# Output projection from the second half of W_out, with its first tiles and gates reordered and the last tile's norm moved among the MLP's sets

## The chip, the core and the metric

The kernel runs on one core of a Trainium2 chip. A core has five engines, each with its own in-order instruction queue: TensorE (PE in the profile; its weight loads are PEld), VectorE (DVE), ScalarE (ACT), GpSimd (POOL) and SyncE (SP). They meet only through semaphores. PE writes to PSUM, from which DVE and ACT read; everything else lies in SBUF. DMA transfers are issued from an engine's queue (here nearly all from SP's) and are carried by 16 shared DMA engines. An instruction that waits holds up everything behind it on its own queue and nothing else. In this kernel the order on every queue is the order in which the Python code issues the instructions.

The metric is device time in microseconds. Before the change it was 3015.29 us, the median of three runs (3013.46 to 3018.35).

## What is computed

One layer of a diffusion backbone, for 256 context tokens and 2048 latent tokens (2304 tokens, 18 tiles of 128). Attention and a Fourier mixing give 512 columns each; this case is about what comes after them:

```python
def merge(attn, four, subln_g, lam_init, w_out):
    a = rms_norm(attn, subln_g) * (1.0 - lam_init)
    return jnp.concatenate([a.reshape(b, n, ATTN_WIDTH), four], axis=-1) @ w_out

mix = merge(attn, fourier_mix(f, w_four[l]), subln_g[l], lam_init, w_out[l])
xs = xs + g1 * mix
h = rms_norm(xs, norm2_g[l]) * (1 + sc2) + sh2
xs = xs + g2 * sq_relu_mlp(h, w1[l], w2[l])        # square(relu(h @ w1)) @ w2
```

The model width is 1024, the MLP's inner width 4096. The context tokens have their own modulation vectors (index `s` = 1, the latent tokens `s` = 0).

## The kernel before, in words

All products are float32 at high accuracy: each operand is split into a rounded part ("h" or "hi", by a cast on ACT or DVE) and the remainder ("l" or "lo", by a subtraction on DVE), and three matmuls replace one (`mm3`, lines 85 to 88).

**Attention** ends first. The last group of rows of the last head transposes its probabilities on PE (`tr`, line 972), splits them (`ah` on ACT, `al` on DVE) and multiplies them with V (`mul`). Then `o1` copies the result out of PSUM, `o2` transposes it back, `o3` copies it to SBUF, `o4` to `o6` normalize it (two squares on ACT, a step on DVE, a power and two scalings on POOL) and store it to `att`. These steps are put in an event list with due times and are sorted by them. W_out (8 blocks `WOUT[k]` of 128 x 1024) has been loaded long before into buffers of a head that is done.

**Output projection** (lines 1304 to 1449). The 18 token tiles go in the order `seq` = 0, 9, 1, 10, ..., 8, 17, so that tile t and tile t + 9 follow each other; the prediction calls the first three s0, s1 and s2. The parts of a tile:

- `mix_load(i)` issues three loads on SP: x (`xo`), the attention part (`am`) and the Fourier part (`mT`).
- `mix(i)` transposes `am` (4 transposes into `pmx`, line 1343), ACT scales that into `mT`, DVE makes `mh` and `ml` (lines 1347 and 1348).
- `w_split(hf)` makes the two parts of one half (512 columns) of W_out: 8 casts on ACT (`woh`), 8 subtractions on DVE (`wol`).
- `out_mm(i, hf)`: 24 matmuls of 128x512, eight k-blocks of three, into one of three PSUM tiles `po`.
- `mk_gate` builds the gate g1 as a row on all partitions: per half 4 matmuls into the single PSUM tile `pg` and a copy on ACT.
- `out_post(i, hf)`: two DVE operations, gate times product and the sum with x. `x_store` writes the new x, `x_norm` makes its RMS norm (ACT square, DVE, POOL power, DVE scaling to `xn`).
- `finish(i)`: 8 transposes of `xn` (`ptb`, line 199), 8 ACT operations to `hTb`; after tile t + 9 POOL makes four sums `ht` of the pair's quarters, and SP stores seven operands `hd` for the MLP.

Before, the first tiles are issued in the order: loads of s0 and s1, `w_split(0)`, `mix(s0)`, `out_mm(s0, 0)`, both halves of the context gate, `mix(s1)`, `w_split(1)`, loads of s2, `out_mm(s1, 0)`, both halves of the other gate, `out_mm(s0, 1)`, and then the loop. Four tiles before the last, the MLP's first loads are put on SP together: two sets of w1 blocks (`w_load`, four loads of 256 KB each, tile `a`) and three operands (`h_load`, 768 KB each, tile `hr`).

**MLP, first product** (lines 1452 to 1665). It uses a scheme with seven products in place of eight per pair of blocks. `ITEMS` lists them: for each set q of hidden columns the products p = 1, 6, (3 of the set before), 2, 7, 5, 4. One product is 12 matmuls of 128x384 (`mms`, lines 1492 to 1494). Products 1 and 2 share PSUM bank A, 6 and 7 bank B, 5 and 3 bank C. The later of two accumulates onto the earlier, so it must wait until the earlier one's result has been read (`post`: `us` on ACT for p = 1, `u` on DVE for p = 6). The weights need sums of blocks (`w_add`, `ws`, DVE), a cast (`w_cast`, ACT) and a remainder (`w_low`, DVE); the operands a cast (`mhh`) and a remainder (`mhl`) once per third of the tokens (`h_prep`). `mlp_ahead` does the first of these among the last tile's output projection.

The last tile's norm and its four sums are not done in the output projection but in `fin_norm` to `fin_store`, at the items 1, 3, 4, 6 and 7 of the MLP; their result is needed only in the last third of the tokens.

**Places.** Tile pools are laid out as two stacks, and a pool that lies where an earlier one lay makes each new tile wait for the readers of the old tiles underneath. Before, the first half of W_out's parts lies in the pool that is opened last on the left side, the second half just behind the working tiles.

## Time and profile before

| | us |
|---|---|
| median of three runs | 3015.29 |
| lowest, highest | 3013.46, 3018.35 |
| profiled execution, its own time | 3011.0 |
| span of that execution in the trace | 3009.2 |

| engine | busy us | share of the span |
|---|---|---|
| PE | 2922.0 | 97% |
| DVE | 2010.9 | 67% |
| ACT | 1568.6 | 52% |
| POOL | 1029.1 | 34% |

In the trace, attention's last matmul starts at 1324.95 us, the output projection's first transpose at 1326.07, the MLP's first matmul at 1582.65, and the last matmul into bank A at 2291.9.

How to read the views: the *timeline* gives start, duration, engine, line, and output <- inputs, with the idle time of that engine ahead of it and what ended it in brackets. The *waits* sum such idle times by who was waited for: total us, times, longest. The *windows* give the engines' busy us in a stretch, then the granted PE clock as a part of full speed (PEclk), the DMA engines' busy share and GB/s. Names are those of the program without numbers. One row of the timeline can hold several like instructions (x8); its duration is then that of the run of them. A matmul's duration includes its way through the array, so that successive ones overlap; the step from one start to the next is what it costs.

### The profile page before, as it was taken

The numbers are of one execution on the slowest core, as the hardware profiler recorded it, in microseconds if no ns is written. First come the engines' busy times: TensorE is split into PE (matmuls) and PEld (weight loads), VectorE is DVE, ScalarE is ACT, GpSimd is POOL, SyncE is SP. The second block draws the span as 40 slices with busy tenths as digits, with TensorE's granted clock in tenths as the row PEclk, the third lists the DMA queues.
The fourth block names the chain that finished last, engine by engine and source line by source line (L and its number), as shares of the span: only waits on it lengthen the run. The fifth ranks groups of instructions, "written<-read, shape, count | busy, mean of one in ns | idle before, by whom it ended". The sixth has DMA issues, their size and how long they took to land.

```text
span 3009.2 us, 43765 instructions
## 1 busy us (share of the span) xinstructions
PE 2922.0 (97%) x15417; PEld 2528.2 (84%) x15417; DVE 2010.9 (67%) x3375; ACT 1568.6 (52%) x3540; POOL 1029.1 (34%) x843
## 2 busy tenths in 40 slices
PE   8999999899999999989998999999999999999999
PEld 5888887678888888877878999999998888888887
DVE  6667775688888888864448777777775335344554
ACT  4333322688888888853336556556555322232221
POOL 1111112189888898831222333333332000000000
PEclk9999999999999999999999999999999999999999
DMA  7777878421121212114676676676666454444563
GB/s 271 208 190 207 221 192 256 176 101 33 46 107 34 107 38 87 32 50 161 199 224 211 229 241 214 213 230 222 222 199 212 150 166 163 131 155 164 200 218 105
DMA packets 394414, 495.58 MB, mean 165 GB/s; under 512 B 26403, under 2 KB 307056, under 8 KB 391122
## 3 DMA queue, kind: packets, MB, share of 16 engines
q1 hardware_dynamic: 386560, 477.63, 49.7%
q0 software_dynamic: 2992, 7.28, 0.8%
q10 hardware_dynamic: 4642, 7.88, 0.8%
q8 instruction: 122, 2.00, 0.3%
q14 instruction: 98, 0.80, 0.1%
HBM read 315.20 MB, written 179.57 MB: 164 GB/s over the span
## 4 chain that ended last, share of the span: by engine, by line
PE 82%; ACT 8%; DVE 4%; DMA 2%; issue 1%; SPq 1%; POOL 0%; ACTq 0%; DVEq 0%; POOLq 0%
PE Ss L916 8%; PE ps L87 8%; PE ps L86 8%; PE ps L88 8%; PE pj L87 4%; PE pj L88 4%; PE pj L86 4%; PE pts L972 3%; ACT P1s L940 3%; PE pB L1492 2%; PE pB L1494 2%; PE pB L1493 2%; PE pA L1492 2%; PE pA L1493 2%; PE pA L1494 2%; PE pC L1494 2%
## 5 line engine op out<-in xcount | busy, mean ns | idle before, releaser
L921 DVE TENSOR_REDUCE mxs<-Ss 128x1 f32<-128x512 f32 x640 | 419.1, 687 | 87.7 <-PE Ss L916 77.2
L1222 DVE TENSOR_TENSOR sl<-sr,sh 128x768 fp32r<-128x768 f32 x168 | 161.0, 959 | 349.4 <-ACT sh L1221 341.2
L963 POOL TENSOR_TENSOR P0s<-P0s,P1s 128x1024 f32<-128x1024 f32 x124 | 365.3, 2946 | 10.3
L1221 ACT CAST sh<-sr 128x768 fp32r<-128x768 f32 x168 | 140.1, 835 | 432.0 <-PE ps L87 432.0
L940 ACT ACTIVATE P1s<-Ss,mxs 128x512 f32<-128x512 f32 x320 | 217.2, 693 | 70.7 <-DVE mxs L924 70.7
L86 PE MATMUL pj<-wh,hh 128*128 128x512 f32 x576 | 229.3, 398 | 0.7 <-ACT fo L374 0.7
L87 PE MATMUL ps<-tlT,sh 128*128 128x512 f32 x585 | 229.3, 392 | 0.0
L86 PE MATMUL ps<-thT,sh 128*128 128x512 f32 x585 | 229.2, 392 | 0.0
L87 PE MATMUL pj<-wl,hh 128*128 128x512 f32 x576 | 227.8, 395 | 0.5 <-DVE wl L496 0.5
L88 PE MATMUL ps<-thT,sl 128*128 128x512 f32 x585 | 227.7, 389 | 0.0
L88 PE MATMUL pj<-wh,hl 128*128 128x512 f32 x576 | 226.5, 394 | 0.0
L1534 POOL TENSOR_TENSOR gs<-g,g 128x384 f32<-128x384 f32 x48 | 70.8, 1475 | 449.9 <-ACT g L1504 389.6
L940 ACT ACTIVATE P0s<-Ss,mxs 128x512 f32<-128x512 f32 x320 | 215.8, 696 | 7.5 <-DVE mxs L924 7.3
L916 PE MATMUL Ss<-KS1s,Qs 128*128 128x512 f32 x640 | 200.8, 427 | 11.4 <-ACT P0s L940 9.6
L916 PE MATMUL Ss<-KS0s,Qs 128*128 128x512 f32 x640 | 197.9, 421 | 10.7 <-ACT P1s L940 9.6
L972 PEld LDWEIGHTS pts<-ident,P0s 128*128 128x128 f32 x1280 | 157.1, 140 | 53.3 <-PE Ss L916 5.6
L972 PE MATMUL pts<-ident,P0s 128*128 128x128 f32 x1280 | 191.8, 273 | 7.4 <-DVE alp L1069 4.0
L1503 ACT ACTIVATE g<-uz 128x384 f32<-128x384 f32 x144 | 75.8, 527 | 207.4 <-DVE uz L1526 183.1
L87 PE MATMUL ps<-oplT,sh 128*128 128x512 f32 x423 | 166.9, 395 | 4.9 <-DVE oplT L1209 4.9
L962 POOL TENSOR_SCALAR P1s<-P1s,tots 128x1024 f32<-128x1024 f32 x124 | 166.7, 1344 | 5.6
L983 DVE TENSOR_TENSOR als<-pts,ahs 128x512 fp32r<-128x512 f32 x256 | 163.8, 681 | 5.4 <-ACT ahs L978 5.3
L86 PE MATMUL ps<-ophT,sh 128*128 128x512 f32 x423 | 166.9, 394 | 0.4 <-DVE uz L1526 0.4
(611 smaller groups left out, 8234.2 us busy)
## 6 DMA issues: line engine op xcount, KB each, us to landing
sr<-sd SPq DMA_DIRECT2D x84, 768.0 KB, 4.5
a<-in_w SPq DMA_DIRECT2D x184, 256.0 KB, 3.8
sd<-gs SPq DMA_DIRECT2D x192, 192.0 KB, 1.9
sd<-g SPq DMA_DIRECT2D x144, 192.0 KB, 4.3
wm<-in_w_mod SPq DMA_DIRECT2D x32, 512.0 KB, 5.0
Qs<-qd SPq DMA_DIRECT2D x32, 512.0 KB, 3.8
b<-in_w SPq DMA_DIRECT2D x64, 256.0 KB, 4.9
b<-tsum SPq DMA_DIRECT2D x64, 256.0 KB, 4.8
```

The source lines that it names most:

```text
L86: nc.tensor.matmul(ps, lh, rh, start=first, stop=False)
L87: nc.tensor.matmul(ps, lh, rl, start=False, stop=False)
L88: nc.tensor.matmul(ps, ll, rh, start=False, stop=last)
L916: nc.tensor.matmul(S[:, :w], self.Q[:, x, m, j * P:j * P + P], self.hd.KS[m][:, b * 512:b * 512 + w], start=(x == 0), stop=(x == 1))
L921: nc.vector.tensor_reduce(self.mx[j][:, m, b:b + 1], self.S[j, m, b], axis=AX.X, op=ALU.max)
L940: nc.scalar.activation(dst, S, AF.Exp, bias=self.mx[j][:, m, 6:7], accum_out=self.sm[j][:, m, b:b + 1])
L962: nc.gpsimd.tensor_scalar(p, p, tot[:, 3:4], 0.0, op0=ALU.mult, op1=ALU.add)
L963: nc.gpsimd.tensor_add(d, d, p)
L972: nc.tensor.transpose(pt[:, c:c + P], self.p0[j][:, (kb + t) * P:(kb + t + 1) * P], ident)
L983: nc.vector.tensor_sub(t, self.pt[kb], f32(self.A[kb][0]))
L1222: nc.vector.tensor_sub(lo, src, f32(hi))
L1494: nc.tensor.matmul(ps, wl[:, c], hh[:, k, :], start=False, stop=k == 3, skip_group_check=True)
```

## The change

- Attention's last group: its `o`, `osq`, `oss` and `s0e` tiles come from another pool, and its steps `o4` to `o6` leave the event list (`LASTO`). They are issued after the first 12 matmuls of the output projection.
- The output projection begins with the second half of W_out. Its parts lie in two pools of their own (`o_wh`, `o_wl`), the mixes in `o_m`, gates and norms in `o_g`. The loads of x are split off (`x_load`) and issued after those of `am` and `mT`. The weights are made in the order in which the matmuls use them: the first block's cast, `mix(s0)` with that block's remainder between `mh` and `ml`, then the other seven blocks. The first half of W_out is made later.
- The gates are built one half at a time, each ahead of its use. Both halves of s0 and s1 are done before the loop.
- The MLP's first loads are spread over the tiles 11 to 15 of the sequence instead of all at tile 14; at tile 15 `w_load(1)` comes after the last tile's loads.
- In the last tile `out_post(i, 0)` comes ahead of `mlp_ahead(0)`, and `mlp_ahead` has three parts; the first set's fourth sum is made there in place.
- The MLP's operands have a pool for each p, in the order 3, 4, 5, 2, 7.
- In the MLP's first items the casts follow a list (`CASTS`), `post(0, 6)` comes ahead of the sums of weights, the sums for the next set move from p = 6 and 2 to p = 7 and 5, and the load of set 2 from p = 7 to p = 5.
- The last tile's norm, transposes, load, sums and stores move from the items 1 to 7 to the items 10 to 22, in smaller pieces; the sums go from POOL to DVE.

```diff
-                    for t, fn in ((0, gr.o1), (0.4, gr.o2), (0.75, gr.o3), (2.32, gr.o4), (3.557, gr.o5), (4.0, gr.o6)):
-                        add(w + t * u, fn)
+                        if gr.last and t > 2:
+                            LASTO.append(fn)
+                        else:
+                            add(w + t * u, fn)
...
-            pool = hpa if p in (1, 6) else hp
+            pool = hpa if p in (1, 6) else hp[p]
...
-                w_cast(2)
-                w_low()
-            else:
+            elif part == 1:
                 for n in range(2):
                     h_load(0, ORDER[n + 3])
+                w_cast(2)
                 w_cast(3)
+            else:
                 w_low()
+                R = RAW[0]
+                nc.vector.tensor_sub(R["a12"], R["a12"], R["s2"])
+                R["s4"] = R["a12"]
...
+            tm = c4.enter_context(tc.tile_pool(name="o_m", bufs=2, reuse_waits="tile"))
+            wl1 = c4.enter_context(tc.tile_pool(name="o_wl", bufs=1, reuse_waits="tile"))
             t4 = c4.enter_context(tc.tile_pool(name="o_t", bufs=2, reuse_waits="tile"))
-            wp = c4.enter_context(tc.tile_pool(name="o_w", bufs=1, reuse_waits="tile"))
+            wh1 = c4.enter_context(tc.tile_pool(name="o_wh", bufs=1, reuse_waits="tile"))
+            tg = c4.enter_context(tc.tile_pool(name="o_g", bufs=2, reuse_waits="tile"))
...
-                mix_load(seq[0])
-                mix_load(seq[1])
+                mix_load(s0)
+                mix_load(s1)
+                x_load(s0)
+                x_load(s1)
+                nc.scalar.copy(WO[1][0][0], WOUT[0][:, 512:1024])
+                mix(s0, lambda: nc.vector.tensor_sub(WO[1][1][0], WOUT[0][:, 512:1024], f32(WO[1][0][0])))
+                w_split(1, 1)
+                out_mm(s0, 1, 0, 4)
+                for fn in LASTO:
+                    fn()
+                mix(s1)
+                out_mm(s0, 1, 4)
+                mk_gate(pp, g1[1], 16, 1, (1,))
                 w_split(0)
-                mix(seq[0])
-                out_mm(seq[0], 0)
-                mk_gate(pp, g1[1], 16, 1)
-                mix(seq[1])
-                w_split(1)
                 kv_even.close()
...
+                mix_load(s2)
+                x_load(s2)
+                out_mm(s1, 1)
+                mk_gate(pp, g1[0], 16, 0, (1,))
+                out_post(s0, 1)
+                out_mm(s0, 0)
+                mk_gate(pp, g1[1], 16, 1, (0,))
+                out_post(s1, 1)
+                mix(s2)
+                out_post(s0, 0)
+                x_store(s0)
+                x_norm(s0)
+                mix_load(seq[3])
+                x_load(seq[3])
+                out_mm(s1, 0)
+                mk_gate(pp, g1[0], 16, 0, (0,))
+                out_post(s1, 0)
+                x_store(s1)
+                x_norm(s1)
+                finish(s0)
+                for n, i in enumerate(seq[2:], 2):
...
-                    if n == N4 - 4:
+                    if n == N4 - 7:
                         w_load(0)
-                        for p in ORDER[:3]:
-                            h_load(0, p)
-                        w_load(1)
+                    if n in (N4 - 6, N4 - 5, N4 - 4):
+                        h_load(0, ORDER[n - N4 + 6])
                     if n == N4 - 3:
                         w_ahead()
+                        w_load(1)
...
-            hp = c5.enter_context(tc.tile_pool(name="m_h", bufs=1, reuse_waits="tile"))
+            hp.update((p, c5.enter_context(tc.tile_pool(name=f"m_h{p}", bufs=1, reuse_waits="tile"))) for p in (3, 4, 5, 2, 7))
...
-                nc.gpsimd.tensor_sub(T[:, 0], b12, b11)
-                nc.gpsimd.tensor_sub(T[:, 1], b22, T[:, 0])
...
+                    nc.vector.tensor_sub(T[:, 0], b12, b11)
+                    nc.vector.tensor_sub(T[:, 1], b22, T[:, 0])
...
-            FINISH = {1: (fin_norm,), 3: (fin_T,), 4: (fin_load,), 6: (fin_sums,), 7: (fin_store,)}
+            FINISH = {10: (fin_norm, ()), 12: (fin_scale, ()), 13: (fin_T, (0,)), 14: (fin_T, (1,)), 15: (fin_T, (2,)),
+                      16: (fin_load, ()), 19: (fin_sums, (0,)), 21: (fin_sums, (1,)), 22: (fin_store, ())}
+            CASTS = ((), (4,), (5,), (8, 6), (7,), (9,), (10, 11))
...
+                    early = q == 0 and p == 6
+                    if early:
+                        post(q, p, ps)
                     nw = q + 1
-                    if p == 1 and wset(q) == q:
+                    if q and p == 1 and wset(q) == q:
                         w_add(q, 3)
                     if nw < NQ and wset(nw) == nw:
-                        for x in {6: (0, 1), 2: (2,)}.get(p, ()):
+                        for x in ({7: (0, 1), 5: (2,)} if q == 0 else {6: (0, 1), 2: (2,)}).get(p, ()):
                             w_add(nw, x)
-                    if p == 7 and q + 2 < NQ and wset(q + 2) == q + 2:
+                    if p == (7 if q else 5) and q + 2 < NQ and wset(q + 2) == q + 2:
                         w_load(q + 2)
-                    post(q, p, ps)
+                    if not early:
+                        post(q, p, ps)
```

One more line shifts a list in the MLP's first third (`TSETS`, the sets beside which sums of w2's blocks are made) by one set.

More of the change, by code (lines that the diff above doesn't have):

```diff
@@ L1352, in x_half, with out_mm @@
                 return XT[i][hf] if i == LAST else XT[i][:, hf * 512:hf * 512 + 512]
-            def out_mm(i, hf):
+            def out_mm(i, hf, k0=0, k1=KD):
                 mh, ml = M[i]
-                po = PS[i, hf] = pp.tile([P, 512], F32, tag="po", name=f"po4_{i}_{hf}", bufs=3)
+                if not k0:
+                    PS[i, hf] = pp.tile([P, 512], F32, tag="po", name=f"po4_{i}_{hf}", bufs=3)
+                po = PS[i, hf]
                 wh, wl = WO[hf]
-                for k in range(KD):
+                for k in range(k0, k1):
                     mm3(po, mh[:, k, :], ml[:, k, :], wh[k], wl[k], k == 0, k == KD - 1)
@@ L1374, in x_norm @@
             def x_norm(i):
-                XN[i] = t4.tile([P, D], F32, tag="xn", name=f"xn{i}")
+                XN[i] = tg.tile([P, D], F32, tag="xn", name=f"xn{i}")
                 norm(t4, XT[i], f"b{i}", XN[i])
```

124 lines of the change are left out of this document (64 added, 60 removed).

## The prediction

> **What bounds the kernel now.** I read the page first, then the windows of the stages that the diff touches, then the waits of PE in them, then the timelines. The page:
>
> ```profile
> span 3009.2 us, 43765 instructions
> PE 2922.0 (97%) x15417; PEld 2528.2 (84%) x15417; DVE 2010.9 (67%) x3375; ACT 1568.6 (52%) x3540; POOL 1029.1 (34%) x843
> ```
>
> PE is the bound, and the change alters none of its work: as many matmuls and transposes as before. It can only win or lose what PE stands still, and what PE loses at a low clock. That is 87 us over the whole span; the windows show which of it is within reach.
>
> ```profile
> 1320.00:1375.00 55.00, 41.49 (x192) 33.56 (x191) 21.95 (x34) 18.96 (x41) 4.09 (x6) 0.84 0.26 89
> 1375.00:1500.00 125.00, 125.00 (x601) 102.81 (x601) 60.48 (x80) 46.38 (x110) 34.44 (x30) 1.00 0.62 200
> 1555.00:1583.00 28.00, 22.04 (x98) 18.22 (x97) 13.21 (x18) 13.77 (x28) 6.06 (x5) 0.88 0.65 195
> 1583.00:1630.00 47.00, 39.44 (x210) 38.13 (x210) 40.11 (x54) 28.70 (x52) 12.14 (x9) 0.93 0.72 221
> ```
>
> The first number after the stretch is its length, the second PE's busy time. From 1375 to 1500, in the projection's steady state, PE is never idle and its clock (the third number from the end) is 1.00. The other three stretches have gaps and a clock of 0.84 to 0.93: the projection's first tiles, its last tile, the MLP's first sets. The waits name the gaps:
>
> ```profile
> PE po L86 <- DVE mh L1347: 7.2, 2, 5.7
> ...
> PE pB L1492 <- DVE u L1516: 7.2, 2, 4.4
> PE pmx L1343 <- DMA am<-att: 6.0, 1, 6.0
> ```
>
> **Part 1, the first tiles.** How they start now:
>
> ```profile
> 1325.53 4.25 ACT L1320 CAST woh<-wout 128x512 fp32r<-128x512 f32 x8
> 1326.07 0.63 PE L1343 MATMUL pmx<-ident,am 128*128 128x128 f32 x4
> 1326.66 4.89 DVE L1321 TENSOR_TENSOR wol<-wout,woh 128x512 fp32r<-128x512 f32 x8
> 1329.99 0.67 ACT L1344 ACTIVATE mT<-pmx,cols 128x512 f32<-128x512 f32 x1
> 1331.54 0.68 DVE L1347 CAST mh<-mT 128x1024 fp32r<-128x1024 f32 x1
> 1332.26 1.23 DVE L1348 TENSOR_TENSOR ml<-mT,mh 128x1024 fp32r<-128x1024 f32 x1
> 1332.37 0.76 PE L86 MATMUL po<-woh,mh 128*128 128x512 f32 x1 [5.67 <-DVE mh L1347]
> ```
>
> ACT makes all eight casts before it comes to `mT`, DVE all eight remainders before `mh`, and PE waits 5.67 us behind them. In the new order ACT has one cast (4.25/8 = 0.53 us) and then `mT` at about 1326.7, when `pmx` is there; it ends at 1327.4, `mh` ends at 1328.1, and PE starts 4.2 us earlier, at 1328.15. One remainder (4.89/8 = 0.61) goes between, so `ml` ends at 1329.95 instead of 1328.7; the other seven follow at 0.61 each and end at 1334.2. A k-block costs PE three matmuls. Their pitch, full clock, and the rows for the later steps:
>
> ```profile
> 1351.22 0.68 DVE L1364 TENSOR_TENSOR gt<-po,g 128x512 f32<-128x512 f32 x1
> 1363.31 1.06 ACT L186 ACTIVATE nsqb<-xo 128x1024 bf16<-128x1024 f32 x1 [6.44 <-DVE xo L1365]
> 1364.74 0.57 POOL L83 TENSOR_TENSOR nrsb<-nssb,mhalf 128x1 f32<-128x1 f32 x1 [28.77 <-DVE nssb L187]
> 1365.35 0.75 DVE L190 TENSOR_SCALAR xn<-xo,nrsb 128x1024 f32<-128x1024 f32 x1 [0.70 <-POOL nrsb L83]
> 1375.05 0.39 PE L86 MATMUL po<-woh,mh 128*128 128x512 f32 x1
> 1376.90 0.39 PE L88 MATMUL po<-woh,ml 128*128 128x512 f32 x1
> ```
>
> Eight steps from 1375.05 to 1376.90: 0.23 us each, 0.69 a block, 5.55 for the 24 of an `out_mm`. Thus DVE (0.61 a block) keeps just ahead of PE. What the clock does is read from windows of 3.4 us:
>
> ```profile
> 1326.90:1330.30 3.40, 0.00 (x0) 0.00 (x0) 3.40 (x7) 3.40 (x9) 0.00 (x0) 1.00 1.00 356
> ...
> 1340.50:1343.90 3.40, 2.55 (x21) 2.12 (x19) 0.00 (x0) 1.16 (x3) 0.00 (x0) 1.00 0.00 0
> 1343.90:1347.40 3.50, 1.59 (x6) 1.03 (x7) 2.83 (x4) 3.50 (x8) 0.00 (x0) 1.00 0.00 0
> 1347.40:1350.80 3.40, 3.40 (x10) 2.65 (x9) 3.40 (x7) 1.24 (x3) 0.00 (x0) 0.50 0.00 0
> ```
>
> After a window with PE busy 1.59 of 3.5 us the clock fell to 0.50 for the next window; after one with 2.55 of 3.4 it held. In the new order the window from 1326.9 holds three matmuls, about 1 us: I take it that the clock falls once, from 1330.3 to 1333.7, and that costs half of it, 1.7 us. The Trainium skill ("TensorE: Matmul & The Clock Gate", "Why this matters for your kernels") tells to avoid idle gaps of more than about 3 us. By that rule the pauses of 1.5 and 0.8 us left here would not bring the clock down, and the sum would be 1.7 us better; the windows shown here are against it.
>
> The steps of PE from there: 12 matmuls to 1333.95, `pmx` of s1 to 1334.4, then the other 12 to 1337.2, with `mh` and `ml` of s1 ready at 1337.05 (ACT `mT` from 1334.4, then 0.67, 0.68, 1.23). Half a gate (4 matmuls) 0.5; `out_mm(s1, 1)` to 1343.3; gate 0.5; `out_mm(s0, 0)` to 1349.35, whose weights ACT and DVE make from 1338.3 to 1343.8, always ahead; gate 0.5; `pmx` of s2 0.4; `out_mm(s1, 0)` to 1355.9; gate 0.5. Then `finish(s0)` needs `xn(s0)`. DVE: two `out_post` (two operations of 0.68 each) done by 1346.6, `mh` and `ml` of s2 at 1353, `out_post(s0, 0)` 1354.4, ACT square and its read-out 1.25, POOL 0.57, `xn` 0.75, small steps: 1357.3. PE waits 0.9 us, and the transposes take 0.9 us. The first matmul of s2 comes at about 1358.5. Before, it comes at 1375.05, after the same work: **a gain of 16 us**. What could be late next: `mT`'s load (SP starts no earlier than before, since the first loads still wait for the probabilities' last transposes underneath, but `am` and `mT` now go ahead of x) and a second window at half clock; 2 and 1.7 us. Own range 12 to 17. No gain comes from `o4` to `o6`: they are off PE's path, their result is read by the last tile only; what they now queue behind costs nobody. The places matter here: the second half's casts lie over probabilities of the group before the last, which are free; the first half, which lies over the last head's V, is made when that is read.
>
> **Part 2, the last tile.** The rows:
>
> ```profile
> 1530.62 0.60 PE L1343 MATMUL pmx<-ident,am 128*128 128x128 f32 x4
> 1543.12 0.60 PE L1343 MATMUL pmx<-ident,am 128*128 128x128 f32 x4
> 1547.39 5.96 SPq L1165 DMA_DIRECT2D a<-in_w x4
> 1556.49 0.36 SPq L1334 DMA_DIRECT2D am<-att x1
> 1561.74 1.09 PE L1343 MATMUL pmx<-ident,am 128*128 128x128 f32 x4 [5.96 <-DMA am<-att]
> 1576.20 1.04 PE L199 MATMUL ptb<-ident,xn 128*128 128x128 f32 x8
> ```
>
> The tiles come every 12.50 us (1530.62 to 1543.12). The last tile's `am` stands behind eight `a` loads and three `hr` loads on SP, is issued at 1556.49 and lands 5 us later; PE waits 5.96 us. The stretch from 1561.74 to the transposes at 1576.20, which has a tile's work, takes 14.46, so 1.96 us more went to the clock. Spread over tiles 11 to 15, with the last four loads behind the last tile's own, nothing is ahead of this `am`: **8 us gained**, own range 6 to 8. Cover: the DMA engines' share in the steady state is 0.62 at 200 GB/s, so 0.38 x 12.5 = 4.7 us of them are free per tile; the largest addition to a tile, 1 MB, takes 1.05 MB / (200/0.62 = 323 GB/s) = 3.3 us.
>
> **Part 3, the MLP's first sets.** PE's losses here:
>
> ```profile
> 1594.33 0.66 PE L1492 MATMUL pB<-mhh,ophW 128*128 128x384 f32 x1 [4.38 <-DVE u L1516]
> ...
> 1609.09 1.78 DVE L1464 TENSOR_TENSOR ws<-a,ws 128x512 f32<-128x512 f32 x1
> 1615.50 0.44 PE L1492 MATMUL pB<-mhh,ophW 128*128 128x384 f32 x1 [2.82 <-DVE u L1516]
> ```
>
> Product 7 must wait until DVE has read product 6 (`u`). At the first place `u` stands behind the last tile's norm and two `ws`; at the second, DVE's sums take 1.78 us while POOL works on the last tile's sums. In the window 1583 to 1630 PE is idle 47 - 39.44 = 7.6 us, and at a clock of 0.93 it loses 0.07 x 47 = 3.3 more: about 10. The norm's and the sums' instructions, with two loads and five stores on SP, move to where PE is bound and the others have room (the steady MLP); I cost them at nothing there. DVE takes over four sums of 512 columns, 0.68 each as `gt` has it. If it had no room, they would cost 2.7 us.
>
> What stays is DVE's own queue. Its rows and the operand's load:
>
> ```profile
> L1271 DVE TENSOR_TENSOR mhl<-hr,mhh x7: 1749/1754/1758, 1577.1 to 1605.5; 128x1536 fp32r<-128x1536 f32 x7
> hr<-hd SPq DMA_DIRECT2D x7, 768.0 KB, 5.5
> ```
>
> From the MLP's first matmul (time 0) DVE has the last `out_post` (1.4), two weight remainders and a sum (3 x 0.68 = 2.0), `mhl` of p = 2 to 4.9 and of p = 7 to 6.6, `u` at 7.1. A product takes PE 12 x 0.17 = 2.1 us, so p = 2 (due 4.2) waits 0.5 for its `mhl`, and p = 7 0.3 for `u`: 4.38 becomes under 1. Then the operand of p = 4: its buffer is free when p = 2's is split (4.9), it lands 5.5 us later, at 10.4, the cast takes 1.5 and `mhl` 1.75: 13.6, where PE is due at 11.4. PE waits 2 us there and 1 more for the weights of set 1, whose remainders stand behind. Left over: 4 to 5 us. Set 2's load moves behind this (SP waits for the buffer of the in-place sum, about time 15, lands at 19 to 20); DVE's sums of it are due at 21. **Gain 5 us**, own range 1 to 9: none if a pause falls into one window and takes the clock down, 9 if the operand's load is early.
>
> **The sum.** 16 + 8 + 5 = 29 us. The profiled execution took 3011.0 us, 1.8 more than its span, and 4.3 less than the median; I take the gain off the median: 3015.3 - 29 = **2986 us**. From the own ranges alone: 2981 (12 of the 34 us is unlikely to be all at its best) to 2996.
>
> **The rivals.**
> - *The clock holds* in part 1, as the skill's rule has it: 1.7 us better, 2984. For it: only pauses below 2 us. Against it: the window with 1.59 us. Chance 0.05.
> - *DVE becomes the bound of the MLP's start.* It is busy 40.1 of 47 us there already, and everything passes through it in order. If the pauses only change their name, part 3 gives nothing and the clock falls once more (1.7): 24 - 2 = 22 us gained, 2993. Chance 0.15.
> - *The head start is lost*: `mT`'s load or a tile's old contents hold `mh` back until about 1332, as now. Then the first wait stays 5.67 with its cold stretch, and part 1 is worth 16 - 6 = 10, the sum 23, or with part 3 failing 16: 2992 to 2999. Against it: the loads have 256 KB ahead of them where they had 768. Chance 0.08.
> - *It does not do what it says*: the waits on SP and DVE are handed on, and the ends stay: no change, 3015. Chance 0.05.
> - *Slower*: the extra load of each of the tiles 11 to 15 delays the next tile's `am` as the last one's was delayed, five times 8.1 = 40 us for the 29 gained: 3026. It decides if the additions need more than the 4.7 us of DMA time that a tile has free (or `am` has over 8 us of delay); 3.3 speaks against it. Chance 0.03.
>
> **How the numbers follow.** The forecast (2980 to 2991) has 0.64. Two runs of this kernel differ by up to 0.16%, so about 0.2% (6 us) can be told from no change. Forecast, holding clock, DVE bound and lost start all lie below 3009: 0.64 + 0.05 + 0.15 + 0.08 = 0.92 faster; no effect 0.05; slower 0.03. The range for 8 in 10 goes from 2980 to 2999: it takes in these four and leaves out the last two and the ends.
>
> **What would show it.** Right: `po` waits for `mh` under 2 us at the start; the first matmul of s2 is about 32 us after the first `pmx`, where it is 49 now; the last tile's `pmx` has no wait for `am` and comes 12.5 us after the one before; `pB` waits for `u` under 1 us in sum, and a wait for `mhl` or a weight remainder of 2 to 4 us stands in the MLP's first 20 us; the `tf` sums are on DVE at 0.7. Wrong: a wait of PE for a load in the tiles 12 to 17; a clock under 0.9 in the MLP's first 15 us; the MLP's first matmul less than 20 us earlier than 1582.65.

## The result, and the profile after

The changed kernel takes 2976.0 us (median of 4 runs, 2972.45 to 2976.96), the kernel before 3014.38 us in the same session (4 runs, 3013.16 to 3018.35). The ratio is 0.9868, with a 95% interval of 0.9851 to 0.9885: 38 us faster, where 29 were forecast, and 4 us under the low end of the range.

The page of the changed kernel, its span and the line of busy times:

```profile
span 2975.1 us, 43755 instructions
PE 2910.2 (98%) x15417; PEld 2518.0 (85%) x15417; DVE 2016.3 (68%) x3379; ACT 1568.3 (53%) x3540; POOL 1023.9 (34%) x839
```

The same 15417 entries on PE, and 12 us less busy time although no matmul is gone: fewer of them ran at a low clock, and many follow each other at a shorter step, as is shown below. The windows, cut at the same events as the four of before (columns as there):

```profile
1320.00:1361.00 41.00, 37.57 (x204) 31.43 (x203) 23.81 (x38) 16.67 (x34) 4.12 (x6) 0.96 0.32 107
1361.00:1486.00 125.00, 125.00 (x608) 103.84 (x607) 60.94 (x81) 49.18 (x118) 34.38 (x30) 1.00 0.67 205
1531.00:1559.00 28.00, 28.00 (x134) 23.14 (x133) 18.11 (x24) 14.24 (x30) 6.87 (x6) 1.00 0.67 206
1559.00:1606.00 47.00, 42.88 (x229) 40.01 (x228) 38.35 (x55) 31.49 (x58) 7.32 (x7) 0.96 0.63 198
```

The first tiles: PE now idles 3.4 us of 41, where it idled 13.5 of 55. The steady state: 608 PE entries in 125 us where there were 601, which the forecast did not have. The last tile: not idle at all. The MLP's first sets: 4.1 us idle of 47, where it was 7.6.

How the first tiles start, from the timeline:

```profile
1327.52 0.60 PE L1357 MATMUL pmx<-ident,am 128*128 128x128 f32 x4
1328.22 0.69 ACT L1358 ACTIVATE mT<-pmx,cols 128x512 f32<-128x512 f32 x1 [1.02 <-PE pmx L1357]
1328.94 0.69 DVE L1361 CAST mh<-mT 128x1024 fp32r<-128x1024 f32 x1 [0.74 <-ACT mT L1358]
1329.55 0.68 DVE L1425 TENSOR_TENSOR wol<-wout,woh 128x512 fp32r<-128x512 f32 x1
1329.78 0.47 PE L86 MATMUL po<-woh,mh 128*128 128x512 f32 x1 [1.66 <-DVE mh L1361]
...
1331.43 0.50 PE L88 MATMUL po<-woh,ml 128*128 128x512 f32 x1 [0.64 <-DVE ml L1364]
...
1360.23 1.09 PE L199 MATMUL ptb<-ident,xn 128*128 128x128 f32 x8 [0.63 <-DVE xn L190]
1361.08 0.48 PE L86 MATMUL po<-woh,mh 128*128 128x512 f32 x1
```

The waits of 1.66, 0.64 and 0.63 us stand where the forecast had 1.5, 0.8 and 0.9, and the last row is s2's first matmul. The last tiles and the MLP's start, from the timeline of PE:

```profile
1527.72 0.60 PE L1357 MATMUL pmx<-ident,am 128*128 128x128 f32 x4
...
1540.10 0.60 PE L1357 MATMUL pmx<-ident,am 128*128 128x128 f32 x4
...
1558.86 0.34 PE L1532 MATMUL pA<-mhh,ophW 128*128 128x384 f32 x1
...
1566.53 0.41 PE L1532 MATMUL pB<-mhh,ophW 128*128 128x384 f32 x1 [0.34 <-DVE u L1556]
...
1573.43 0.45 PE L1533 MATMUL pD<-mhl,ophW 128*128 128x384 f32 x1 [1.35 <-DVE mhl L1276]
```

No wait for `am` before the last `pmx`, 12.38 us after the one before it. `pB` waits 0.34 for `u`, and the longest wait is the forecast one for p = 4's operand.

The rest is found by cutting both executions at the same events: attention's first transposes of a result (`o2`, in the profile `pos<-ident,oTs`), the first `pmx`, s2's first matmul, the MLP's first, the second product's first, in the second product the first with a `thT` operand, and the last matmul. Lengths in us; "again" is a second profiled execution of the kernel before:

| stretch | before | before, again | after | gain | forecast |
|---|---|---|---|---|---|
| attention: first `pos<-ident,oTs` to first `pmx` | 692.13 | 692.22 | 688.26 | 3.9 | none |
| head: first `pmx` to s2 | 48.98 | 49.08 | 33.56 | 15.4 | 16 |
| tail: s2 to the MLP | 207.61 | 207.37 | 197.77 | 9.8 | 8 |
| MLP's first product | 717.69 | 717.54 | 714.48 | 3.2 | 5 |
| second product to `thT` | 26.98 | 27.17 | 19.90 | 7.1 | none |
| from there to the last matmul | 677.11 | 677.11 | 677.11 | 0 | none |

The gains sum to 39.4 us. The two executions themselves differ by 34.1, because the changed kernel's came to the first of these events 5.3 us later; the two rows (before, then after) are:

```profile
633.94 0.38 PE L1006 MATMUL pos<-ident,oTs 128*128 128x128 f32 x2
...
639.26 0.38 PE L1008 MATMUL pos<-ident,oTs 128*128 128x128 f32 x2
```

Two gains stand where the forecast has no term: 3.9 us in attention, of which the experiment with part 1 alone tells more, and 7.1 us in the second product, which the change does not touch. There the kernel before shows, in windows and timeline:

```profile
2310.00:2313.40 3.40, 0.00 (x0) 0.00 (x0) 0.49 (x1) 1.08 (x3) 0.00 (x0) 1.00 0.64 240
2313.40:2320.20 6.80, 5.67 (x13) 4.45 (x14) 5.82 (x9) 0.00 (x0) 0.00 (x0) 0.50 0.59 171
```

```profile
2307.14 1.29 SPq L1546 DMA_DIRECT2D sd<-gs  x2
...
2312.91 0.96 DVE L1222 TENSOR_TENSOR sl<-sr,sh 128x768 fp32r<-128x768 f32 x1 [7.65 <-DMA sd<-gs]
...
2314.53 0.79 PE L87 MATMUL ps<-oplT,sh 128*128 128x512 f32 x1 [4.89 <-DVE oplT L1209]
```

DVE's `sl`, an operand of the second product, waits 7.65 us for the store of a `gs` tile issued 5.8 us before; `oplT` stands behind it on DVE's queue, PE waits 4.89 for that, a window without any matmul passes, and the clock stays at 0.50 for two windows. The changed kernel's DVE, at the same place:

```profile
2275.14 0.68 DVE L1214 TENSOR_TENSOR oplT<-b,ophT 128x512 fp32r<-128x512 f32 x1
2277.10 2.85 DVE L1227 TENSOR_TENSOR sl<-sr,sh 128x768 fp32r<-128x768 f32 x2 [1.27 <-ACT sh L1226]
```

No store is waited for. Worked out from the pools: in the kernel before, `fin_norm` takes two `gs` tiles for the unused output of its squares at the MLP's second item, before most other tiles of that pool exist. The `gs` buffers therefore lie from byte 5120 of the pool, and the second product's pool, which starts at the same place, puts its `sl` at 3072 to 6144. In the changed kernel those squares go into `xnf`, and the first `gs` tile is taken later and lies higher.

### The profile page after: what moved, and what is told of

It is laid out like the page before. It is cut to its first block, busy times and chain, and to the rows that moved or that the text cites. A ratio compares the mean times of both kernels' runs of the same rounds, so it can differ in the third digit from the quotient of the medians.

```text
span 2975.1 us, 43755 instructions
## 1 busy us (share of the span) xinstructions
PE 2910.2 (98%) x15417; PEld 2518.0 (85%) x15417; DVE 2016.3 (68%) x3379; ACT 1568.3 (53%) x3540; POOL 1023.9 (34%) x839
## 4 chain that ended last, share of the span: by engine, by line
PE 84%; ACT 8%; DVE 4%; DMA 2%; issue 1%; POOL 0%; SPq 0%; ACTq 0%; DVEq 0%; POOLq 0%
PE Ss L918 8%; PE ps L86 8%; PE ps L87 8%; PE ps L88 8%; PE pj L86 4%; PE pj L88 4%; PE pj L87 4%; PE pts L974 4%; ACT P1s L942 3%; PE po L88 2%; PE po L86 2%; PE po L87 2%; PE pA L1532 2%; PE pA L1534 2%; PE pA L1533 2%; PE pC L1534 2%
## 5 line engine op out<-in xcount | busy, mean ns | idle before, releaser
L88 PE MATMUL ps<-ophT,sl 128*128 128x512 f32 x423 | 165.7, 392 | 0.0
```

Source lines behind the costliest of these rows:

```text
L88: nc.tensor.matmul(ps, ll, rh, start=False, stop=last)
```

## The experiments

All times are beside the kernel before on the same chip; its medians were 3013.9 to 3016.1 us. What comes ahead of attention's first `pos<-ident,oTs` varies between executions (633.5 to 639.3 us in fourteen, with the changed kernel's at the upper end), so the lengths of the stretches say more than medians of different sessions. Stretches that a run leaves alone mostly repeat within about 0.3 us, or differ by one to three where windows of low clock fall in or out.

| kernel | median | ratio (95%) | attention | head | tail | MLP | to `thT` |
|---|---|---|---|---|---|---|---|
| before, `gs` moved | 3008.33 | 0.9973 (0.9963 to 0.9984) | 692.13 | 48.50 | 207.55 | 720.15 | 19.23 |
| after, `gs` put back | 2980.31 | 0.9880 (0.9866 to 0.9893) | 688.42 | 33.54 | 197.77 | 713.38 | 27.01 |
| after, loads together | 2978.00 | 0.9872 (0.9859 to 0.9886) | 688.38 | 33.53 | 203.68 | 713.11 | 19.91 |
| after, last norm back | 2977.83 | 0.9870 (0.9857 to 0.9883) | 690.08 | 34.07 | 197.77 | 718.50 | 19.23 |
| before with part 1 | 2993.56 | 0.9929 (0.9917 to 0.9942) | 688.21 | 33.55 | 205.67 | 718.18 | 27.64 |
| after, eight casts first | 2977.26 | 0.9878 (0.9864 to 0.9891) | 689.19 | 36.96 | 197.75 | 714.12 | 19.91 |
| after, places of before | 2976.70 | 0.9876 (0.9862 to 0.9889) | 688.26 | 33.58 | 199.63 | 713.71 | 19.91 |
| after, gate early | 2973.60 | 0.9862 (0.9847 to 0.9877) | 688.36 | 32.51 | 197.77 | 714.86 | 19.91 |
| places of before, rotated | 2976.81 | 0.9875 (0.9858 to 0.9891) | 688.28 | 33.42 | 199.63 | 715.47 | 19.92 |
| gate early, rotated | 2974.12 | 0.9866 (0.9851 to 0.9881) | 690.00 | 31.13 | 197.77 | 714.55 | 19.90 |
| after, pools swapped | 2975.88 | 0.9876 (0.9848 to 0.9905) | 687.96 | 34.27 | 198.92 | 714.02 | 19.90 |

**The `gs` tiles moved in the kernel before.**

```diff
+                xn = f32(hp.tile([P, 4, 384], F32R, tag="mhh3", name="xnf")).rearrange("p a b -> p (a b)")
...
-                    junk = t5.tile([P, 384], F32, tag="gs", ..., bufs=4).bitcast(mybir.dt.bfloat16)[:, 0:512]
-                    nc.scalar.activation(junk, XT[LAST][hf], AF.Square, ...)
+                    nc.scalar.activation(xn[:, hf * 512:hf * 512 + 512], XT[LAST][hf], AF.Square, ...)
...
-                xn = f32(hp.tile([P, 4, 384], F32R, tag="mhh3", name="xnf")).rearrange("p a b -> p (a b)")
```

> The kernel before, in which only the discarded output of the last tile's two squares goes into xnf's own buffer instead of two gs buffers; so the pool of the MLP's working tiles hands out its places in another order, and the gs buffers no longer lie where the second product's first sl tile is put. Theory (places): DVE's sl no longer waits 7.65 us for the store of a gs tile, PE's wait of 4.89 us for oplT and the cold stretch behind it are gone, the kernel is 7 us faster than before (ratio 0.9977) and the step from the first matmul with ophT to the first with thT is 20 us instead of 27. Rival (the stores only land earlier in the changed kernel because its stages before are shorter): the wait stays, no change (ratio 1.000).

Measured: 7.8 us faster, and the stretch to `thT` is 19.23 instead of 26.98. PE's waits from 2264 to 2330 us, in a single line:

```profile
PE ps L86 <- DVE uz L1526: 0.4, 1, 0.4
```

The wait for `oplT` is gone; the MLP is 2.5 us longer, with one more window of low clock than before. Nothing else of the change is in this kernel, so the rival falls.

**The `gs` tiles put back in the changed kernel.**

```diff
+                nc.gpsimd.memset(t5.tile([P, 512], F32, tag="ws3", ...)[:, 0:8], 0.0)
...
+                    if n == 1:
+                        for x in range(2):
+                            nc.gpsimd.memset(t5.tile([P, 384], F32, tag="gs", ..., bufs=4)[:, 0:8], 0.0)
```

> The changed kernel, in which one ws3 tile and two gs tiles are taken (with a memset of 8 columns on POOL) before the MLP's first tiles of these pools, so that the places are handed out as in the kernel before. Theory (places): the wait of sl for the store of a gs tile is back, PE waits about 5 us for oplT, and the kernel is 7 us slower than the changed one (about 2983). Rival (the start of the second product is faster for another reason): no wait, within 2 us of the changed kernel (2976).

The stretch to `thT` is 27.01 us, 7.1 longer, and the waits of DVE and PE are those of before:

```profile
DVE sl L1227 <- DMA sd<-gs: 8.1, 1, 8.1
...
PE ps L87 <- DVE oplT L1214: 4.7, 1, 4.7
```

The median is 4 us over the changed kernel's, not 7; it was taken in another session, and what comes ahead of attention alone varies by more. By the stretch, the place is shown in both directions.

**The loads together again.**

```diff
-                    if n == N4 - 7:
+                    if n == N4 - 4:
                         w_load(0)
-                    if n in (N4 - 6, N4 - 5, N4 - 4):
-                        h_load(0, ORDER[n - N4 + 6])
+                        for p in ORDER[:3]:
+                            h_load(0, p)
+                        w_load(1)
                     if n == N4 - 3:
                         w_ahead()
-                        w_load(1)
```

> The changed kernel with the MLP's first loads put back together at tile 14 (both w1 sets around three operands), behind them the last tile's own loads. Theory (the prediction's part 2): the last tile's pmx waits again about 6 us for am, with a cold stretch of 2 us behind: 6 to 8 us slower than the changed kernel. Rival (the tail gained by the faster step of the matmuls alone, or by what the new places allow): no wait for am, within 2 us of the changed kernel.

The timeline of SP, then PE's last `pmx`:

```profile
1523.55 3.40 SPq L1170 DMA_DIRECT2D a<-in_w  x4
1526.99 1.45 SPq L1183 DMA_DIRECT2D hr<-hd  x3
1528.49 5.90 SPq L1170 DMA_DIRECT2D a<-in_w  x4
1534.49 2.35 SPq L1348 DMA_DIRECT2D am<-att  x1
...
1541.28 1.09 PE L1357 MATMUL pmx<-ident,am 128*128 128x128 f32 x4 [4.39 <-DMA am<-att]
```

`am` is issued behind eleven loads, PE waits 4.39 us, and the tail is 5.9 us longer, though the median is only 2.0 us higher. Of the 9.8 us that the tail gained, 5.9 are the spreading's (wait and cold stretch). By the stretch the theory holds, just under its 6 to 8, and the rival, which has no such wait, falls; the medians of the two sessions do not show the difference.

**The last tile's norm and sums back at the items 1 to 7, sums on POOL.**

```diff
-            FINISH = {10: (fin_norm, ()), 12: (fin_scale, ()), 13: (fin_T, (0,)), ..., 22: (fin_store, ())}
+            FINISH = {1: ((fin_norm, ()), (fin_scale, ())), 3: ((fin_T, (0,)), (fin_T, (1,)), (fin_T, (2,))),
+                      4: ((fin_load, ()),), 6: ((fin_sums, (0,)),), 7: ((fin_store, ()),)}
...
-                nc.vector.tensor_sub(T[:, 0], b12, b11)
+                nc.gpsimd.tensor_sub(T[:, 0], b12, b11)
```

> The changed kernel with the last tile's norm, transposes, load, sums and stores put back at the MLP's items 1, 3, 4, 6 and 7, and the sums back on POOL; all other edits of the MLP's start stay. Theory (the prediction's part 3: these steps stood before the reads that PE waits for): waits of pB for u of 4 to 7 us in sum come back, 3 to 5 us slower than the changed kernel. Rival (VectorE's queue bounds the MLP's first sets in any order, and the move gave nothing): within 1.5 us of the changed kernel.

The MLP is 4.0 us longer (the median, of another session, 1.8), and the two waits for `u` are back. From the timelines of PE, DVE and POOL:

```profile
1567.55 0.41 PE L1532 MATMUL pB<-mhh,ophW 128*128 128x384 f32 x1 [2.41 <-DVE u L1556]
...
1574.86 0.69 DVE L1504 TENSOR_TENSOR ws<-a,a 128x512 f32<-128x512 f32 x1
...
1582.13 1.78 DVE L1504 TENSOR_TENSOR ws<-a,ws 128x512 f32<-128x512 f32 x1
1583.32 1.73 POOL L1631 TENSOR_TENSOR hf<-hf 128x512 f32<-128x512 f32 x1
1583.83 3.43 DVE L1258 TENSOR_TENSOR oplW<-ws,ophW 128x512 fp32r<-128x512 f32 x2
...
1589.24 0.69 PE L1532 MATMUL pB<-mhh,ophW 128*128 128x384 f32 x1 [4.61 <-DVE u L1556]
```

The second wait comes from DVE's own instructions: a sum that takes 0.69 alone takes 1.78 while POOL works on its sums, two remainders 3.43. The Trainium skill ("SBUF — State Buffer", "Who interferes with whom") says that a DVE instruction with two inputs in SBUF contends with a GpSimd instruction that reads SBUF; these rows agree. The move alone is worth 4.0 us, more than all of part 3 (3.2): the other edits of the MLP's start, taken together, brought nothing that these runs show.

**Part 1 alone, in the kernel before.** The projection's section of the changed kernel, with the loads, the last tile's order and the whole MLP as before.

> The kernel before with part 1 alone: the new order and places of the output projection's first tiles, gates and attention's last steps; the MLP's first loads together as before, the last tile's and the MLP's orders as before. Theory (the parts add up): the stretch from the first pmx to the first matmul of s2 shrinks from 49.0 to about 33.6 us, the stretch from there to the MLP's first matmul by no more than the 1.9 us that the shorter step of the matmuls gives, and the wait for oplT in the second product stays: 15 to 17 us faster than before (ratio about 0.9945). Rival (what the first tiles win is given back at the last tile, where the loads are late anyway): under 12 us faster.

Faster by 0.71% (0.58% to 0.83%), 17.5 to 25 us. The head is 33.55, the tail 205.67, and PE's waits behind it are those of before:

```profile
PE pB L1526 <- DVE u L1550: 7.2, 2, 4.1
PE ps L87 <- DVE oplT L1213: 5.7, 1, 5.7
PE pmx L1353 <- DMA am<-att: 4.9, 1, 4.9
```

Nothing is given back later, and the tail's 1.9 us come with part 1, without any loads spread. But the gain is over the 15 to 17 of the theory, and the stretches named there cannot make it up. The rest is in attention: 688.21 us with part 1 alone, where the kernels with attention as before have 692.13, 692.22 and 692.13. It is no single wait: at the 17th `pos<-ident,oTs` row of the 32, half of it is there (365.40 us after the first before, 363.41 in the changed kernel), and PE idles no less (16.1 us before, 17.1 after). PE's steps are shorter: at full clock and without idle time, successive `Ss<-KS1s` start 271.2 instead of 274.7 ns apart, a `pos<-als` and the matmul behind it 116.4 instead of 118.4. In attention's code part 1 changes only the pool of the last group's four tiles and the time of its last steps; since the gain is spread over the whole stage, and stays with the projection's places of before (688.26, below), it must come from what the pool shifts. That is argued; no run has this edit alone.

**All eight casts and remainders first.**

```diff
-                nc.scalar.copy(WO[1][0][0], WOUT[0][:, 512:1024])
-                mix(s0, lambda: nc.vector.tensor_sub(WO[1][1][0], ...))
-                w_split(1, 1)
+                w_split(1)
+                mix(s0)
```

> The changed kernel with one step of the order undone: all eight casts and remainders of the second half of W_out are issued ahead of the mix of s0, as before the change for the first half. Theory (the prediction's step: mT and mh stood behind eight casts and eight remainders): PE waits 5 to 6 us for the first mh instead of 1.7, and the stretch from pmx to s2 is 37.5 to 39.5 us instead of 33.6. Rival (the start is bound by the loads of am and mT or by old contents of the places, not by the order): 33 to 35 us.

The head is 36.96, between the two. The timelines of ACT, DVE and PE show why:

```profile
1321.61 4.27 ACT L1332 CAST woh<-wout 128x512 fp32r<-128x512 f32 x8
...
1327.08 4.90 DVE L1333 TENSOR_TENSOR wol<-wout,woh 128x512 fp32r<-128x512 f32 x8
1327.18 0.69 ACT L1358 ACTIVATE mT<-pmx,cols 128x512 f32<-128x512 f32 x1 [1.03 <-PE pmx L1357]
1331.89 0.69 DVE L1361 CAST mh<-mT 128x1024 fp32r<-128x1024 f32 x1
1332.72 0.76 PE L86 MATMUL po<-woh,mh 128*128 128x512 f32 x1 [5.64 <-DVE mh L1361]
```

ACT makes its eight casts before `pmx` is there and holds `mT` up not at all; in the kernel before the first half's casts began only at 1325.53. The half that goes first matters on ACT, the order of the remainders on DVE.

**The places of before under the new order.**

```diff
-            tm = c4.enter_context(tc.tile_pool(name="o_m", ...))
-            wl1 = c4.enter_context(tc.tile_pool(name="o_wl", ...))
             t4 = c4.enter_context(tc.tile_pool(name="o_t", ...))
-            wh1 = c4.enter_context(tc.tile_pool(name="o_wh", ...))
-            tg = c4.enter_context(tc.tile_pool(name="o_g", ...))
+            wp = c4.enter_context(tc.tile_pool(name="o_w", ...))
+            tm, tg, wh1, wl1 = t4, t4, wp, wp
```

> The changed kernel with the new order of the first tiles, but the places of the output projection's tiles as before: one pool behind the working tiles for gates and both parts of the second half of W_out, the mixes and norms back in the working pool. Theory 1 (the new order needs the new places: the second half's remainders would lie over tiles that attention reads to its end): the first remainders wait, the stretch from pmx to s2 is 2 to 6 us longer than 33.6. Theory 2 (the step between two matmuls goes with the places): it is back at 0.2333 us on average in the projection, the stretch from s2 to the MLP is 1.9 us longer (199.7 instead of 197.8). Rival: places matter for neither, 33.6 and 197.8.

The head is the same (33.58): theory 1 falls, the second half needs no new places to start. Theory 2 holds: the tail is 199.63, the step about 233.2 ns, and the tiles follow each other every 12.50 us as in the kernel before, where the changed kernel has 12.38:

```profile
1402.65 0.60 PE L1355 MATMUL pmx<-ident,am 128*128 128x128 f32 x4
1415.15 0.60 PE L1355 MATMUL pmx<-ident,am 128*128 128x128 f32 x4
```

**The first half gate in PE's first wait.**

```diff
                 mix(s0, lambda: nc.vector.tensor_sub(WO[1][1][0], ...))
+                mk_gate(pp, g1[1], 16, 1, (1,))
                 w_split(1, 1)
...
                 out_mm(s0, 1, 4)
-                mk_gate(pp, g1[1], 16, 1, (1,))
```

> The changed kernel with the first half gate (4 matmuls, 0.5 us of PE) issued between the first pmx and the first matmul, where PE waits 1.7 us for mh, instead of after the first out_mm. Theory (the clock falls after a window of 3.4 us in which PE is busy for less than about half): the busy time of that window rises from 1.9 to 2.4 us, the clock holds, the stretch from pmx to s2 is 2.0 to 2.2 us shorter (31.4). Rival 1 (only the 0.5 us are moved, the clock falls all the same): 33.0. Rival 2 (the gate's copy delays the casts on ACT by 0.6, and the matmuls wait for them): 33.6 to 34.2.

The head is 32.51, 1.05 us shorter, and the clock fell all the same: neither value, nearest to rival 1. The windows around the start:

```profile
1326.10:1329.50 3.40, 1.99 (x10) 1.18 (x10) 2.72 (x4) 3.25 (x7) 0.00 (x0) 1.00 0.85 320
1329.50:1332.90 3.40, 3.40 (x9) 2.52 (x9) 3.40 (x7) 2.33 (x8) 0.00 (x0) 0.52 0.75 264
```

**The kernel before, profiled again**, unchanged.

> The kernel before, profiled a second time. Its profiled execution took 3011.0 us, 3 to 5 less than its medians (3014.4 to 3016.1), so the traces account for 34 us of a gain of 38. Theory 1 (the number of cold stretches of PE's clock varies between executions): this execution takes 3013 to 3018 us, has one to three more stretches of 3.4 us at half clock than the first, each worth up to 1.7 us, in the stages ahead of the output projection or at the changed places, and the unchanged stretches are otherwise equal within 0.5 us. Theory 2 (the loads are slower in some executions): the waits for DMA at the start or in attention are longer and the clock is the same.

3012.9 us, with the same stretches of low clock and the same lengths within 0.25 us; the first `pmx` comes 2.0 us later, of which 1.9 lie ahead of attention's first `pos<-ident,oTs`. Neither theory holds, and the premise falls too: the traces account for 39 us, once attention is counted.

**Remainders rotated: the places of before, and with the early gate.** A block's remainder lies 18432 instead of 16384 bytes behind its cast, in both halves in the first kernel and in the first half in the second (there the second half's remainders lie low).

```diff
+                    for k in (KD - 1, *range(KD - 1)) if x == "l" else range(KD):
+                        WO[hf][n][k] = q.tile([P, 512], F32R, tag=f"wo{x}{hf}_{k}", ...)
```

> As p_places (the changed kernel's order, the places of before), but in both halves the eight remainders of W_out lie in the order 7, 0, 1, ..., 6, so that a block's remainder lies 18432 instead of 16384 bytes behind its cast, as in the second product's operands, where a step takes 0.2289 us on average. Theory 1 (the step of the matmuls goes with the distance between the two parts of a block, and 16384 is a bad one): 0.229 us in both halves, the stretch from s2 to the MLP is 196 to 197 us. Theory 2 (the low place of the second half's remainders made them faster, or something else than the distance): 0.2332 as in p_places, 199.6 us.

> The changed kernel with the first half gate ahead of the first matmul (as in g_gate_early) and the remainders of both halves in the order 7, 0, 1, ..., 6. If the distance between a block's two parts sets the step (theory 1): both halves at 0.229 or below, the stretch from s2 to the MLP 0.8 to 1.5 us shorter than 197.77, the kernel 1 us faster than g_gate_early. If not (theory 2): as g_gate_early, 197.8 and 2973.6.

Tails of 199.63 and 197.77: theory 1 falls in both. But the second kernel's head is 31.13, with the order of the early gate that gave 32.51. Its windows, cut at its own events:

```profile
1325.70:1329.10 3.40, 2.54 (x21) 2.15 (x20) 0.90 (x2) 1.42 (x3) 0.00 (x0) 1.00 1.01 310
1329.10:1332.50 3.40, 2.39 (x7) 1.34 (x8) 3.40 (x6) 3.40 (x8) 0.00 (x0) 1.00 0.61 239
1332.50:1335.90 3.40, 3.40 (x18) 2.83 (x17) 3.40 (x7) 2.76 (x8) 0.48 (x1) 1.00 0.65 231
```

The same waits, 0.67 and 0.63 us, fell into two windows instead of one, and the clock held: 1.4 us for the same instructions in the same order. So the early gate makes the head 1.05 or 2.4 us shorter, as the windows fall. Both versions lie some 2 us under the changed kernel by their medians, less than the runs of either spread.

**The second half's pools swapped**, casts low, remainders behind:

```diff
-            wl1 = c4.enter_context(tc.tile_pool(name="o_wl", ...))
+            wh1 = c4.enter_context(tc.tile_pool(name="o_wh", ...))
             t4 = c4.enter_context(tc.tile_pool(name="o_t", ...))
-            wh1 = c4.enter_context(tc.tile_pool(name="o_wh", ...))
+            wl1 = c4.enter_context(tc.tile_pool(name="o_wl", ...))
```

> The changed kernel with the two pools of the second half of W_out swapped and nothing else moved: the casts (woh) lie low, at 35616 bytes, the remainders (wol) at 86944. In the changed kernel the steps of the second half from L86, L87, L88 are 232.7, 225.9 and 228.2 ns. Theory 1 (a low place is read faster): the two matmuls that read woh (L86 and L88) become the fast ones, wol's the slow one; the stretch from s2 to the MLP is 197.8 us or less. Theory 2 (it only matters that the two parts of a block lie far apart, with other tiles between): a mean of 229 ns and 197.8 us, as in the changed kernel. Theory 3 (only the remainders' low place matters): 233.2 in the mean, 199.6 us, as with the places of before.

A tail of 198.92, tiles every 12.44 us, and steps of 233.0, 231.4 and 231.5 ns: none of the three theories. That the step between matmuls goes with the places is shown by this kernel and the one with the places of before; by which rule stays open.

## Why the prediction was wrong

**The step that failed is what the sum was taken over.** The prediction says of PE: "It can only win or lose what PE stands still, and what PE loses at a low clock", and adds up "16 + 8 + 5 = 29 us" from three stretches. What these three terms stood for came to 26.5 us (15.4, 7.9 and 3.2). Another 12.9 us came from two things that have no term in it.

The first is a wait in a stage that the change does not touch: 7.1 us in the second product. The prediction looked at places only where weights were made ("The places matter here"); that the squares of the last tile's norm no longer take `gs` tiles moves the buffers of a whole pool, and with them the tile that DVE waits for 700 us later. The row was there to be read: `ps` waiting 4.89 us for `oplT` is among the longest waits of the kernel before. That it goes with the place of the `gs` tiles is shown by the two experiments with them, 7.75 us one way and 7.1 the other.

The second is PE's own step, which the quoted sentence leaves out: with other places the same matmuls follow each other faster, 1.9 us in the tail and 3.9 in attention. For the tail the runs with the places changed show it. For attention the shorter step is shown, and that part 1 brings it; which of its edits does is argued. No row of before could have given either.

That the three forecast stretches sum to 28.4 us, so near 29, is luck: the 1.9 in the tail and the 1.8 that part 3 fell short cancel.

**Part 1, 16 us: right, 15.4.** Waits, half clock for one window and the chain to `xn(s0)` came as worked out. A half gate costs PE 0.81 us (1338.77 to 1339.58 in the timeline, where its 4 matmuls are 8 entries) where 0.5 were put in. The reason given was half right: on ACT nothing stood in the way once the second half goes first; the eight remainders on DVE did (the experiment with the casts first). It is the choice of the half that frees ACT, not the new places: with the old ones the head is 33.58.

**Part 2, 8 us: 7.9 of the 9.8.** The wait and its cold stretch came to 5.9 when put back; another 1.9 is the shorter step of the matmuls (199.63 against 197.77 with the places alone changed), where the tile cadence of 12.50 us was taken as fixed. The remaining 2 us are the difference between part 1 alone (205.67) and the loads together (203.68), both with the wait for `am`: at that wait the clock stayed low for two windows in the one and for one in the other, and the wait was 0.5 shorter. Whether the new order of the last tile did that, or only the way the windows fell, no run tells.

**Part 3, 5 us: mis-sized, 3.2.** The forecast set "about 10" us of waits and clock against "4 to 5" left over. The waits came so: `pB` waits 0.8 in sum instead of 7.2, new ones stand at p = 4, and in windows of 47 us PE idles 4.1 us instead of 7.6. Two costs had no term. The clock fell once more:

```profile
1329.00:1332.40 3.40, 1.94 (x6) 1.00 0.74 293
...
1571.30:1574.70 3.40, 1.55 (x6) 1.00 0.21 59
1574.70:1578.10 3.40, 3.40 (x12) 0.51 0.38 106
```

These windows have PE alone (busy, clock, DMA share, GB/s). The first row is the forecast fall in part 1. Around the wait for p = 4's operand PE was busy 1.55 of 3.4 us, and the next window ran at half clock. The prediction had this as a way to lose part 3; it is not the whole of what is missing, for in four runs without this fall the same MLP still takes 713.11 to 714.86 us.

The other cost is that a wait takes more than its idle time. At the wait of 0.34 us for `u` the starts are 1565.85, 1566.53 and 1566.78: two steps of 0.93 us together, where two without a wait take 0.35, so some 0.25 us are lost beside the idle time. Three waits, two of them long, became eight short ones. Summed step by step over the MLP's first 50 us, PE lost 12.1 us before: 7.5 idle, 2.0 at half clock, 1.0 beside the waits and 1.6 on the last tile's transposes. In the changed kernel it lost 9.0: 4.1, 1.5, 2.7 and 0.7.

**The rivals.** The clock did not hold in part 1. Of the rival with DVE as the bound, half came: the waits that stay in the MLP's first 40 us are all but one for DVE, and the clock fell once more, but part 3 still gave 3.2 us. The head start was not lost, and the spread loads delayed no tile: the cadence is 12.38 to the last one.

**Open:** by the stretches the gain is 39.4 us, by the medians 38 (95%: 35 to 45), so nothing large is missing. What makes the start of an execution, ahead of attention's results, vary by up to 6 us, no run here shows; nor which edit shortens the step in attention, nor the rule by which places set it.

## What to carry to other kernels

A tile that is taken earlier, later or not at all shifts all the buffers that its pool lays out after it, and what a later stage puts over them inherits their waits; look at every wait for a store in the profile, and ask which tile lies underneath, before summing up a change. Sum up by stretches between events that both kernels have, and over the whole execution, not only where the change is: they repeat within tenths of a microsecond where whole executions differ by several. A wait in the middle of work costs its length, here some 0.25 us beside it, and, where it empties most of a clock window, 1.4 us (the two heads) to 2.2 (the second product, 7.1 for a wait of 4.89) behind it.

## What the runs showed of the hardware

The granted clock goes by fixed windows of 3.41 us, not by pauses. In the trace of the kernel before it changed at 1330.36, 1337.19, 1347.43 and 1350.84 us, 2, 3 and 1 such windows apart, and so on to the end. With PE busy 1.55, 1.94 and 1.99 us of a window it fell to half for the next, with 2.06, 2.39 and 2.54 it held, and the longest pause in the window of 1.99 was 0.67. Neither busy time nor the pause decides alone: in the kernel before, a window with 1.58 busy and a pause of 1.83 held (from 1613.67); with part 1 alone, one with 2.15 busy and no pause over 0.63 fell (from 1327.53). The Trainium skill ("TensorE: Matmul & The Clock Gate", "What's actually happening") says that the window is free-running, so that the same kernel meets it at different phases; the two heads of 32.51 and 31.13 us agree.

The step from one matmul of 128x512 to the next in the projection, at full clock and with nothing waited for, was 233.2 ns on average with the places of before and 230.6 with the new ones, within 0.2 ns the same in every kernel with the same places. In the second half of W_out the three steps of a block are 232.7, 225.9 and 228.2 ns with the new places (means of successive starts), while the kernel before alternates between 229 and 238. Neither a distance of 16384 bytes nor the low place alone explains it.
